# The local attention's scores: each head in its own half of the array's rows

## The chip, the cores and the metric

The kernel runs on one core of a Trainium2 chip. The metric is the time of one execution in device microseconds (us); lower is better. TensorE is written PE, its weight loads PEld, VectorE DVE, ScalarE ACT, GpSimd POOL and the queue engine SP.

## The reference, cut to what matters

One decoder layer: a mixing sub-layer of four branches (gated recurrence, dilated local attention, state-space model, cross-attention into 256 memory tokens) and a gated MLP, on 512 positions of width 1024 in float32. The change touches the local attention alone. It has twelve heads of 64 features, in three groups of four heads with (window, dilation) = (128, 1), (512, 4), (2048, 16):

```python
s = jnp.einsum('znqhe,znkhe->znhqk', qs, kb).astype(f32) * (E ** -0.5)
bias = -(slopes * dil)[:, None, None] * dist.astype(f32)
s = jnp.where(valid[None, :, None], s + bias[None, None], -jnp.inf)
m = jnp.max(s, axis=-1, keepdims=True)
p = jnp.exp(s - m)
l = jnp.sum(p, axis=-1, keepdims=True)
o = jnp.einsum('znqhk,znkhe->znqhe', p, vb.astype(f32)) / l.transpose(0, 1, 3, 2, 4)
```

The score of a query and a key of one head is thus a sum over 64 features. After the reordering by dilation there are 4 query tiles of 128 per group. In group 0 a tile sees 256 keys (the first tile 128), in groups 1 and 2 it sees 128.

## The kernel before, in words

Every large product is made in three passes to keep float32 accuracy: an operand is split by ACT and DVE into a high part (rounded to fp32r, the array's own format) and a low part (the rest), and the passes are high x high, high x low, low x high. `wload` (line 75) does that for a weight tile (`whi`, `wlo`), `split` (line 92) for an activation, `mm3` (line 83, its matmul on line 90) makes the 24 matmuls of a "unit": 128 output features by 512 positions, contracted over 8 blocks of 128.

The attention runs in two halves (`Attention(0)` and `Attention(1)`), each with two heads of every group: the 128 rows of a q, k or v unit are two heads of 64. For each group `units_v`, `units_q` and `units_k` make the units; `scores` makes the scores, their bias, maxima and exponentials; `turns` transposes the probabilities on PE (`ptr`, line 558); `values` multiplies them with v (`ops`, line 572; each head writes its own 64 rows of the bank). `run` writes the order out: scores of group g stand between the v and the q unit of group g+1, and for group 2 between units of other work (`fill`: the `glu` units in the first half, `merge` units with their `gate` and `prj` in the second). `weigh` and `combine` join the groups (`rows`, line 586; `bc`, lines 610 and 611, contracted over 2 rows).

Before the change, k is kept twice (`units_k`): with the second head's rows zeroed, and with the first head's, by a split scaled with the columns of `half` (lines 99 and 100). One score matmul (line 531) then contracts all 128 rows against both copies: the output holds both heads' scores side by side, so it has 2w columns for w keys per head. There are 3 passes per query tile. Group 0's four tiles each have a bank and an SBUF tile of their own; in groups 1 and 2 two query tiles share one bank. DVE adds the bias and takes the maximum per tile and head (line 534, with a read-out of the accumulated maximum to `col`), negates the maxima (line 541), and ACT takes the exponential (line 543).

The program takes eight PSUM banks, four under the tag `mm` (units, `ops`) and four under `ax` (scores, transposes and the rest). The program is written in one order, and a planner then orders each engine's instructions by its own estimate of when operands and buffers come free; it may put other matmuls ahead of one that still waits.

Of the kernel before, what the change touches and what calls it, by code (L numbers as in the profile page):

```python
# [12 lines left out]
F32 = mybir.dt.float32  # L13
F32R = mybir.dt.float32r
# [36 lines left out]
def _body(ctx, tc, nc, D):  # L51
# [4 lines left out]
    V, S, G, PE = nc.vector, nc.scalar, nc.gpsimd, nc.tensor  # L56

    def pool(name, bufs=1, side=None):
        return tc.tile_pool(name=name, bufs=bufs, side=side, reuse_waits="tile")
# [4 lines left out]
    def axb(name):  # L64
        return ps.tile([128, 512], F32, tag="ax", name=name)

    def f32(t):
        return t.bitcast(F32)
# [8 lines left out]
    def wload(src, n, raw=None):  # L77
        raw = wfetch(src, n) if raw is None else raw
        hi = wp.tile([128, 1024], F32R, tag="whi", name="whi")
        lo = wp.tile([128, 1024], F32R, tag="wlo", name="wlo")  # L80
        cut[:] = (S.copy(hi[:, :n], raw[:, :n]),  # L81
                  V.tensor_tensor(out=lo[:, :n], in0=raw[:, :n], in1=f32(hi[:, :n]), op=ALU.subtract))  # L82
        return hi, lo
# [9 lines left out]
    def split(hi, lo, src, scale=None, eng=V):  # L93

        if scale is None:
            a = S.copy(hi, src)
            b = eng.tensor_tensor(out=lo, in0=src, in1=f32(hi), op=ALU.subtract)
        else:
            a = S.activation(hi, src, AF.Identity, scale=scale)
            b = V.scalar_tensor_tensor(out=lo, in0=src, scalar=scale, in1=f32(hi), op0=ALU.mult, op1=ALU.subtract)  # L100
        return a, b
# [5 lines left out]
    half = cp.tile([128, 2], F32, name="half")  # L107
# [5 lines left out]
    def rstd_of(pool, s0, s1, n, tag, bufs=1, between=None, eng=V):  # L113

        t, y, e, r = (pool.tile([128, n], F32, tag=tag + x, name=tag + x, bufs=bufs) for x in "tyer")
        if s1 is None:
            eng.tensor_scalar(out=t, in0=s0, scalar1=EPS * DM, scalar2=None, op0=ALU.add)
        else:
            eng.tensor_scalar(out=t, in0=s0, scalar1=s1, scalar2=EPS * DM, op0=ALU.add, op1=ALU.add)
        S.activation(y, t, AF.Sqrt, scale=1.0 / DM)  # L120
        if between is not None:
            between()
        V.reciprocal(y, y)
        if n == 1:
            eng.tensor_scalar(out=e, in0=y, scalar1=y, scalar2=t, op0=ALU.mult, op1=ALU.mult)
        else:
            eng.tensor_tensor(out=e, in0=y, in1=y, op=ALU.mult)
            eng.tensor_tensor(out=e, in0=e, in1=t, op=ALU.mult)
        eng.tensor_scalar(out=e, in0=e, scalar1=-0.5 / DM, scalar2=1.5, op0=ALU.mult, op1=ALU.add)
        eng.tensor_tensor(out=r, in0=y, in1=e, op=ALU.mult)  # L130
        return r
# [52 lines left out]
    def t2(name, dt=F32):  # L184
        return tp.tile([128, 512], dt, tag="t2", name=name)

    def unit(u, nm):
        w = wload(D["w_in"][u], 1024)
        b = mmb(nm)
        mm3(b, w, hT, KC)  # L190
        return b


    with pool("np") as npool:
# [48 lines left out]
        for u in range(6):  # L243
            w = wk[u] if u < 3 else wload(D["mem_wk"][u], 1024)
# [5 lines left out]
            b = (axb if u % 2 else mmb)("kv")  # L250
# [7 lines left out]
        for n in range(3):  # L258
            bv = [mmb("kv") for _ in range(2)]
            for kh in range(2):  # L260
                whi, wlo = wv.pop() if wv else wload(D["mem_wv"][2 * n + kh], 1024)
                for o, passes in enumerate((((1, whi), (0, whi)), ((0, wlo),))):
                    for k in range(4):
                        cs = slice(k * 256, k * 256 + 256)
                        for t in range(2):
                            for a, w in passes:
                                done = PE.matmul(bv[t][:, :256], mT[a][:, 4 * kh + k, t * 128:(t + 1) * 128], w[:, cs],  # L267
                                                 start=(kh == k == o == 0 and a == 1), stop=(kh == 1 and k == 3 and o == 1))
# [28 lines left out]
    with pool("lru", bufs=2) as lp, pool("lruc") as lc:  # L297
# [4 lines left out]
        ab, e, s, s2, q, chf, nch = (sm("lr%d" % i) for i in range(7))  # L302
# [21 lines left out]
        for i0 in range(0, 6, 2):  # L324
            xc, gg, tr, ti = {}, {}, {}, {}
            for i in (i0, i0 + 1):
                b = unit(U_XA + i, "xa")
# [3 lines left out]
                c = xc[i] = lt("xc")  # L331
# [3 lines left out]
            for i in (i0, i0 + 1):  # L335
                b = unit(U_GA + i, "ga")
                gg[i] = lt("gg")
                S.activation(gg[i], b, AF.Gelu_apprx_tanh)
            for i in (i0, i0 + 1):
                for wt, bt, dst, nm in ((wa, ba, tr, "tr"), (wx, bx, ti, "ti")):  # L340
                    b = axb(nm)
# [19 lines left out]
        for i in range(6):  # L361
            b = unit(U_US + i, "us")
# [11 lines left out]
    for i in range(6):  # L374
        b = unit(U_XQ + i, "xq")
        split(xq[:, 0, i], xq[:, 1, i], b)
    PIECES = [[(0, 0, 128), (1, 0, 64)], [(1, 64, 64), (2, 0, 128)], [(3, 0, 128), (4, 0, 64)], [(4, 64, 64), (5, 0, 128)]]
    with pool("xap") as xp:
        for h in range(4):
            P = []  # L380
            for t0 in (0, 2):
                b = axb("xs")
                for j in range(2):
                    t = t0 + j
                    for n, (ch, p0, pn) in enumerate(PIECES[h]):
                        i = ch - (ch + 1) // 3 if pn == 128 else 4 + ch // 3 * 2 + p0 // 64
                        for o, (x, y) in enumerate(((0, 1), (1, 0), (0, 0))):
                            PE.matmul(b[:, j * 256:(j + 1) * 256], xq[:, x, ch, t * 128:(t + 1) * 128], kx[:, y, i],
                                      start=(n == 0 and o == 0), stop=(n == 1 and o == 2))
# [4 lines left out]
                p = t2("xp")  # L394
# [9 lines left out]
            for kb in range(2):  # L404
                b = axb("xpt")
                for t in range(4):
                    PE.transpose(b[:, t * 128:(t + 1) * 128], P[t // 2][:, (t % 2) * 256 + kb * 128:(t % 2) * 256 + kb * 128 + 128], ident)
                p = (t2("xpTh", F32R), t2("xpTl", F32R))
# [51 lines left out]
    ap = apx.enter_context(pool("at"))  # L460
# [6 lines left out]
    def perm_in(g, t):  # L467
        if g == 0:
            return t
        d = 4 if g == 1 else 16  # L470
        return t.rearrange("p (j r) -> p r j", r=d)

    def perm_as(g, t):
        if g == 0:
            return t
        d = 4 if g == 1 else 16
        return t.rearrange("p (r j) -> p r j", r=d)

    class Attention:
# [30 lines left out]

        def units_k(self, g):
            b = unit(U_K + 2 * g + self.h2, "k")

            t = self.k[g] = tuple(ap.tile([128, 2, 512], F32R, tag="k" + s, name="k%d%s" % (g, s), bufs=2) for s in "hl")
            for h in range(2):
                split(perm_as(g, t[0][:, h]), perm_as(g, t[1][:, h]), perm_in(g, b), scale=half[:, h:h + 1])

        def scores(self, g):
            segs = self.segs[g] = []
            if g == 0:  # L520
                parts = [[(0, 0, 128)]] + [[(t, 128 * t - 128, 256)] for t in (1, 2, 3)]
            else:
                parts = [[(t, t * 128, 128) for t in (t0, t0 + 1)] for t0 in (0, 2)]
            for prt in parts:
                new = []
                b = axb("sc")
                st = ap.tile([128, 512], F32, tag="sc", name="sc", bufs=6)
                c = 0
                for (t, k0, w) in prt:
                    for n, (x, y) in enumerate(((0, 1), (1, 0), (0, 0))):  # L530
                        PE.matmul(b[:, c:c + 2 * w].rearrange("p (h k) -> p h k", h=2), self.q[g][:, x, t * 128:(t + 1) * 128],
                                  self.k[g][y][:, :, k0:k0 + w], start=(n == 0), stop=(n == 2))
                    for h in range(2):
                        V.tensor_tensor_reduce(out=st[:, c:c + w], in0=b[:, c:c + w],
                                               in1=self.ab[g][:, h, 256 - w:256] if g == 0 else self.ab[g][:, h, :],
                                               scale=1.0, scalar=-3e38, op0=ALU.add, op1=ALU.max,
                                               accum_out=self.mcol[:, g, t, h:h + 1])
                        new.append((t, h, k0, w, st, c))
                        c += w
                t0, t1 = prt[0][0], prt[-1][0] + 1  # L540
                V.tensor_scalar(out=self.nmc[:, g, t0:t1], in0=self.mcol[:, g, t0:t1], scalar1=-1.0, scalar2=None, op0=ALU.mult)
                for (t, h, k0, w, st, c) in new:
                    S.activation(st[:, c:c + w], st[:, c:c + w], AF.Exp, bias=self.nmc[:, g, t, h:h + 1],
                                 accum_out=self.lcol[:, g, t, h:h + 1])
                segs += new
# [144 lines left out]
    with pool("wo") as wo:  # L690
# [104 lines left out]
        for u in range(3):  # L795
            w = wload(D["ffn_w_up"][u], 1024)
            b = (axb if u % 2 else mmb)("up")
# [3 lines left out]
        w = tuple(x1p.tile([128, n], F32R, name="we" + s)[:, :1024] for s, n in (("h", 1024), ("l", 1048)))  # L801
        with tc.issue_after(done.ins):
            split(*w, wfetch(D["ffn_w_up"][3]))
        b = axb("up")
# [25 lines left out]
    for i in range(24):  # L830
# [4 lines left out]
        c = fp.tile([128, 512], F32, tag="fc", name="fc", bufs=2)  # L835
# [17 lines left out]
    for kb in range(10):  # L853
        for nh in range(2):
            w = wload(D["ffn_w_down"][kb * 2 + nh], 1024)
# [15 lines left out]
    for t in range(4):  # L871
        sc = cols[:, 8 + 2 * t:10 + 2 * t]
        yg = []

        def gained(nh):
            y = fp.tile([128, 512], F32, tag="gs", name="fyg", bufs=2)
            V.tensor_tensor(out=y, in0=acc[t, nh], in1=gmo[:, nh * 512:nh * 512 + 512], op=ALU.mult)
            yg.append(y)
# [5 lines left out]
        r = rstd_of(fp, sc[:, 0:1], sc[:, 1:2], 1, "fo", 4, lambda: gained(1))  # L884
# [396 lines left out]
```

## Time and profile before

| | |
|---|---|
| median of 3 runs | 1183.03 us (1182.72 to 1184.81) |
| the profiled execution | 1185.61 us |
| its span, first to last instruction | 1183.8 us |
| PE busy | 1163.4 us, 98% of the span |
| PEld, DVE, ACT, POOL busy | 82%, 58%, 44%, 11% |
| granted TensorE clock, mean | 0.996 of 2.4 GHz |
| first and last score matmul | 442.5 us, 610.7 us |

The profiled execution lies 2.6 us above the median, and 1.8 us of it lie outside the span. "Busy" of PE counts from a matmul's start to its modelled end, and matmuls are pipelined: one of 512 columns lasts 0.389 us while the next starts 0.227 us later. How much time a matmul takes is therefore read from the chain of waits, whose pieces follow each other without overlap, or from the distance between two starts. Float32 matmuls (`ops`) leave two records each, fp32r matmuls one.

### The profile page before, as it was taken

The numbers are of one execution on the slowest core, as the hardware profiler recorded it, in microseconds if no ns is written. First come the engines' busy times: TensorE is split into PE (matmuls) and PEld (weight loads), VectorE is DVE, ScalarE is ACT, GpSimd is POOL, SyncE is SP. The second block draws the span as 40 slices with busy tenths as digits, with TensorE's granted clock in tenths as the row PEclk, the third lists the DMA queues.
The fourth block names the chain that finished last, engine by engine and source line by source line (L and its number), as shares of the span: only waits on it lengthen the run. The fifth ranks groups of instructions, "written<-read, shape, count | busy, mean of one in ns | idle before, by whom it ended". The sixth has DMA issues, their size and how long they took to land.

```text
span 1183.8 us, 15153 instructions
## 1 busy us (share of the span) xinstructions
PE 1163.4 (98%) x5786; PEld 969.0 (82%) x5786; DVE 687.7 (58%) x1249; ACT 522.8 (44%) x869; POOL 124.6 (11%) x163
## 2 busy tenths in 40 slices
PE   8999999998999999999999999999999999999997
PEld 8977788877788887888888888898888888888886
DVE  6857794588888534486447465585545444432224
ACT  6678734553434235443543234455444443422122
POOL 3000200196651000000000000010000000000000
PEclk9999999999999999999999999999999999999999
DMA  7612442213223322223122323713232323333221
GB/s 288 215 59 71 151 141 63 68 52 96 78 82 114 100 89 67 86 77 112 61 80 64 107 87 118 267 38 107 92 102 92 107 90 94 102 92 104 91 88 71
DMA packets 44296, 120.21 MB, mean 102 GB/s; under 512 B 9630, under 2 KB 13808, under 8 KB 44224
## 3 DMA queue, kind: packets, MB, share of 16 engines
q1 hardware_dynamic: 42432, 115.73, 30.1%
q0 software_dynamic: 1072, 2.46, 0.7%
q10 hardware_dynamic: 720, 1.06, 0.2%
q8 instruction: 45, 0.74, 0.2%
q14 instruction: 27, 0.22, 0.1%
HBM read 115.21 MB, written 4.01 MB: 101 GB/s over the span
## 4 chain that ended last, share of the span: by engine, by line
PE 88%; DVE 7%; DMA 1%; issue 1%; ACT 1%; POOL 1%; DVEq 0%; SPq 0%; ACTq 0%; POOLq 0%
PE up L791 22%; PE gate L90 12%; PE dn L852 11%; PE prj L90 7%; PE glu L90 4%; PE v L90 3%; PE k L90 3%; PE q L90 3%; PE xa L90 3%; PE us L90 3%; PE xq L90 3%; PE ga L90 3%; PE wo L711 2%; PE kv L267 1%; PE kv L90 1%
## 5 line engine op out<-in xcount | busy, mean ns | idle before, releaser
L82 DVE TENSOR_TENSOR wlo<-wraw,whi 128x1024 fp32r<-128x1024 f32 (+1 forms) x198 | 230.6, 1168 | 276.9 <-ACT whi L81 137.3
L81 ACT CAST whi<-wraw 128x1024 fp32r<-128x1024 f32 (+1 forms) x198 | 194.7, 986 | 332.0 <-PE dn L852 71.2
L791 PE MATMUL up<-h2l,whi 128*128 128x512 f32 (+1 forms) x400 | 148.9, 377 | 0.0
L791 PE MATMUL up<-h2h,whi 128*128 128x512 f32 (+1 forms) x400 | 148.7, 376 | 0.0
L90 PE MATMUL gate<-hTh,whi 128*128 128x512 f32 x256 | 101.1, 395 | 0.0
L90 PE MATMUL gate<-hTl,whi 128*128 128x512 f32 x256 | 100.5, 392 | 0.0
L791 PE MATMUL up<-h2h,wlo 128*128 128x512 f32 (+1 forms) x400 | 93.6, 376 | 0.0
L791 PEld LDWEIGHTS up<-h2l,whi 128*128 128x128 f32 x400 | 75.2, 188 | 13.9
L791 PEld LDWEIGHTS up<-h2h,whi 128*128 128x128 f32 x400 | 75.3, 188 | 13.8
L791 PEld LDWEIGHTS up<-h2h,wlo 128*128 128x128 f32 x400 | 72.3, 188 | 13.7
L90 PE MATMUL gate<-hTh,wlo 128*128 128x512 f32 x256 | 63.6, 389 | 0.0
L852 PE MATMUL dn<-whi,aTh 128*128 128x512 f32 x160 | 62.2, 389 | 0.0
L852 PE MATMUL dn<-whi,aTl 128*128 128x512 f32 x160 | 62.2, 389 | 0.0
L90 PEld LDWEIGHTS gate<-hTh,whi 128*128 128x128 f32 x256 | 48.1, 188 | 9.9 <-issue 0.5
L90 PEld LDWEIGHTS gate<-hTh,wlo 128*128 128x128 f32 x256 | 47.9, 188 | 9.8
L90 PEld LDWEIGHTS gate<-hTl,whi 128*128 128x128 f32 x256 | 48.1, 188 | 9.4
L841 DVE TENSOR_TENSOR fc<-fc,up 128x512 f32<-128x512 f32 x24 | 16.5, 687 | 57.6 <-PE up L791 56.5
L852 PE MATMUL dn<-wlo,aTh 128*128 128x512 f32 x160 | 39.5, 389 | 0.0
L290 DVE SCALAR_TENSOR_TENSOR th<-th,prj 128x512 f32<-128x512 f32 x24 | 16.4, 685 | 37.1 <-PE prj L90 36.8
L838 DVE SCALAR_TENSOR_TENSOR fc<-gs,fcw,fc 128x512 f32<-128x512 f32 x48 | 36.1, 751 | 1.5
L852 PEld LDWEIGHTS dn<-whi,aTl 128*128 128x128 f32 x160 | 30.0, 188 | 6.2
L852 PEld LDWEIGHTS dn<-wlo,aTh 128*128 128x128 f32 x160 | 30.0, 188 | 6.2
(517 smaller groups left out, 2439.9 us busy)
## 6 DMA issues: line engine op xcount, KB each, us to landing
wraw<-w_in SPq DMA_DIRECT2D x74, 512.0 KB, 3.5
wraw<-ffn_w_up SPq DMA_DIRECT2D x48, 512.0 KB, 3.4
wraw<-ffn_w_down SPq DMA_DIRECT2D x24, 512.0 KB, 3.5
wraw<-proj SPq DMA_DIRECT2D x24, 384.0 KB, 3.0
wraw<-ssm_glu SPq DMA_DIRECT2D x12, 384.0 KB, 3.0
wraw<-w_out SPq DMA_DIRECT2D x8, 512.0 KB, 4.3
wraw<-mem_wk SPq DMA_DIRECT2D x6, 512.0 KB, 6.8
wraw<-mem_wv SPq DMA_DIRECT2D x6, 512.0 KB, 4.2
```

Source lines behind the costliest of these rows:

```text
L81: cut[:] = (S.copy(hi[:, :n], raw[:, :n]), V.tensor_tensor(out=lo[:, :n], in0=raw[:, :n], in1=f32(hi[:, :n]), op=ALU.subtract))
L82: V.tensor_tensor(out=lo[:, :n], in0=raw[:, :n], in1=f32(hi[:, :n]), op=ALU.subtract))
L90: last = PE.matmul(out, a[:, k * 128:(k + 1) * 128], x[i][:, k], start=(n == 0), stop=(n == 3 * nk - 1))
L267: done = PE.matmul(bv[t][:, :256], mT[a][:, 4 * kh + k, t * 128:(t + 1) * 128], w[:, cs], start=(kh == k == o == 0 and a == 1), stop=(kh = ...
L290: V.scalar_tensor_tensor(out=th, in0=th, scalar=1.0, in1=b, op0=ALU.add, op1=ALU.mult)
L711: PE.matmul(b, mT[k][a][:, ts_], w[p][:, k % 2, :], start=(k == a == p == 0), stop=(k == 7 and p == 1))
L791: PE.matmul(b[:, cs], a[:, k * 128:(k + 1) * 128], x[:, k, cs], start=(n == k == 0), stop=(n == len(order) - 1 and k == KC - 1))
L838: V.scalar_tensor_tensor(out=c, in0=gs[:, j:j + 512], scalar=fcw[:, i, j:j + 1], in1=c, op0=ALU.mult, op1=ALU.add)
L841: V.tensor_tensor(out=c, in0=c, in1=bv, op=ALU.mult)
L852: PE.matmul(acc[t, nh], aT[a][:, k, ts_], w[p][:, cs], start=(k == a == p == 0), stop=(k == 23 and p == 1))
```

## The change

`units_k` makes one split without a mask, so k is kept once, with each head in its own 64 rows. In `scores` every matmul becomes two, one per head: each contracts 64 rows, given by `tile_position=(64 * h, 0)` the upper or lower half of the array's rows, and writes its w columns to that head's own bank. A part now has two banks and two SBUF tiles, one per head. Group 0 has two parts of two query tiles, groups 1 and 2 have one part of four query tiles; the number of banks taken per group is as before. The negation of the maxima is made once per part.

```diff
--- before.py
+++ after.py
@@ -510,33 +510,34 @@
 
         def units_k(self, g):
             b = unit(U_K + 2 * g + self.h2, "k")
-
-            t = self.k[g] = tuple(ap.tile([128, 2, 512], F32R, tag="k" + s, name="k%d%s" % (g, s), bufs=2) for s in "hl")
-            for h in range(2):
-                split(perm_as(g, t[0][:, h]), perm_as(g, t[1][:, h]), perm_in(g, b), scale=half[:, h:h + 1])
+            t = self.k[g] = tuple(ap.tile([128, 2, 512], F32R, tag="k" + s, name="k%d%s" % (g, s), bufs=2)[:, 0] for s in "hl")
+            split(perm_as(g, t[0]), perm_as(g, t[1]), perm_in(g, b))
 
         def scores(self, g):
             segs = self.segs[g] = []
             if g == 0:
-                parts = [[(0, 0, 128)]] + [[(t, 128 * t - 128, 256)] for t in (1, 2, 3)]
+                parts = [[(0, 0, 128), (1, 0, 256)], [(2, 128, 256), (3, 256, 256)]]
             else:
-                parts = [[(t, t * 128, 128) for t in (t0, t0 + 1)] for t0 in (0, 2)]
+                parts = [[(t, t * 128, 128) for t in range(4)]]
             for prt in parts:
                 new = []
-                b = axb("sc")
-                st = ap.tile([128, 512], F32, tag="sc", name="sc", bufs=6)
+
+                b = [axb("sc") for _ in range(2)]
+                st = [ap.tile([128, 512], F32, tag="sc", name="sc", bufs=6) for _ in range(2)]
                 c = 0
                 for (t, k0, w) in prt:
                     for n, (x, y) in enumerate(((0, 1), (1, 0), (0, 0))):
-                        PE.matmul(b[:, c:c + 2 * w].rearrange("p (h k) -> p h k", h=2), self.q[g][:, x, t * 128:(t + 1) * 128],
-                                  self.k[g][y][:, :, k0:k0 + w], start=(n == 0), stop=(n == 2))
+                        for h in range(2):
+                            r = slice(64 * h, 64 * h + 64)
+                            PE.matmul(b[h][:, c:c + w], self.q[g][r, x, t * 128:(t + 1) * 128], self.k[g][y][r, k0:k0 + w],
+                                      start=(n == 0), stop=(n == 2), tile_position=(64 * h, 0))
                     for h in range(2):
-                        V.tensor_tensor_reduce(out=st[:, c:c + w], in0=b[:, c:c + w],
+                        V.tensor_tensor_reduce(out=st[h][:, c:c + w], in0=b[h][:, c:c + w],
                                                in1=self.ab[g][:, h, 256 - w:256] if g == 0 else self.ab[g][:, h, :],
                                                scale=1.0, scalar=-3e38, op0=ALU.add, op1=ALU.max,
                                                accum_out=self.mcol[:, g, t, h:h + 1])
-                        new.append((t, h, k0, w, st, c))
-                        c += w
+                        new.append((t, h, k0, w, st[h], c))
+                    c += w
                 t0, t1 = prt[0][0], prt[-1][0] + 1
                 V.tensor_scalar(out=self.nmc[:, g, t0:t1], in0=self.mcol[:, g, t0:t1], scalar1=-1.0, scalar2=None, op0=ALU.mult)
                 for (t, h, k0, w, st, c) in new:
```

## Rows read from the trace of the kernel before

**Rows 1.** The profile page, parts 1 and 4: busy engines, the chain that ended last.

```profile
PE 1163.4 (98%) x5786; PEld 969.0 (82%) x5786; DVE 687.7 (58%) x1249; ACT 522.8 (44%) x869; POOL 124.6 (11%) x163
...
PE 88%; DVE 7%; DMA 1%; issue 1%; ACT 1%; POOL 1%; DVEq 0%; SPq 0%; ACTq 0%; POOLq 0%
```

**Rows 2.** Busy us (instructions) in one stretch: PE, PEld, DVE, ACT, POOL; clock; DMA share.

```profile
420.00:640.00 220.00, 219.91 (x1121) 179.66 (x1120) 117.27 (x239) 97.03 (x199) 2.09 (x4) 1.00 0.26 81
```

**Rows 3.** Chain, first attention half: start us, length us, engine, tile, line, count.

```profile
425.88 5.44 PE q L90 x24
...
431.76 5.49 PE k L90 x24
...
442.69 2.42 PE sc L531 x12
...
460.06 0.66 PE v L90 x2
460.72 0.37 PE ops L572 x4
461.09 5.23 PE v L90 x22
466.32 0.71 PE sc L531 x6
467.04 0.93 PE q L90 x4
467.97 0.50 PE sc L531 x3
...
480.21 1.02 PE ops L572 x16
```

**Rows 4.** Timeline, 491 to 492 us: start, length, engine, line, operation, idle before, releaser.

```profile
491.49 0.27 DVE L534 CUSTOM_DVE_ANT_0 sc<-sc,ab 128x128 f32<-128x128 f32 x1
...
491.69 0.28 DVE L534 CUSTOM_DVE_ANT_0 sc<-sc,ab 128x128 f32<-128x128 f32 x1
491.90 0.08 DVE L534 DVE_READ_ACCUMULATOR2_ANT col<- 128x1 f32 x1
...
492.04 0.19 PEld L531 LDWEIGHTS sc<-k2l,q 128*128 128x128 f32 x1 [0.51 <-DVE col L534]
```

**Rows 5.** Who waited for whom, 420 to 625 us: us in total, times, longest.

```profile
PEld sc L531 <- DVE col L534: 1.0, 3, 0.5
```

**Rows 6.** The tile ops: duration in ns min/median/max, first and last start.

```profile
L572 PE MATMUL ops<-pt,v x120: 272/273/324, 457.3 to 630.1; 128*64 128x128 f32 x120
```

**Rows 7.** Timeline of weight loads (PEld), behind ops and at bc.

```profile
459.99 0.19 PEld L90 LDWEIGHTS v<-hTh,whi 128*128 128x128 f32 x1 [0.17 <-issue]
460.10 0.19 PEld L90 LDWEIGHTS v<-hTl,whi 128*128 128x128 f32 x1
...
546.91 0.18 PEld L610 LDWEIGHTS bc<-wr,selr 2*128 2x128 f32 x1 [0.17 <-issue]
547.02 0.18 PEld L611 LDWEIGHTS bc<-wr,selr 2*128 2x128 f32 x1
```

**Rows 8.** Chain, second half, at bc.

```profile
546.99 0.42 PE bc L610
...
547.64 0.23 PE bc L610
...
548.57 5.69 PE k L90 x24
```

**Rows 9.** The tile k: splits of group 0's keys.

```profile
L99 ACT ACTIVATE k0h<-k,half x4: 688/690/692, 437.4 to 556.6; 128x512 fp32r<-128x512 f32 x4
L100 DVE SCALAR_TENSOR_TENSOR k0l<-k,half,k0h x4: 743/746/752, 438.5 to 557.4; 128x512 fp32r<-128x512 f32 x4
```

**Rows 10.** The tile xq: a split without a mask.

```profile
L96 ACT CAST xq<-xq x6: 586/589/590, 163.8 to 191.0; 128x512 fp32r<-128x512 f32 x6
L97 DVE TENSOR_TENSOR xq<-xq x6: 679/682/683, 166.5 to 192.2; 128x512 fp32r<-128x512 f32 x6
```

## The prediction

> **What bounds the kernel now.** I read the page first: PE is busy for 98% of the span and holds 88% of the chain that ended last [rows 1]. Then the stretches: from 420 to 640 us, where both attention halves run, PE is busy for 219.91 of 220 us, DVE for 117.27, ACT for 97.03, DMA a quarter [rows 2]. There the reader is to see that time moves only if PE's time does. So I took the chain of waits through the first attention half, where every piece of PE has its length [rows 3]: a unit of 24 matmuls of 512 columns is 5.44 us, 0.227 us each; the twelve score matmuls of group 0 take 2.42 us; six of 256 columns take 0.71 us, 0.118 us each. Group 0 has three of 256 and nine of 512, so one of 512 takes (2.42 - 3 x 0.118)/9 = 0.229 us. Both halves together have 54 of 256 columns and 18 of 512: 54 x 0.118 + 18 x 0.229 = 10.5 us, the whole of what the change rewrites on PE.
>
> The same rows show how they stand in PE's order: group 0's twelve lie in one piece, group 1 in pieces of six, three and three, with q matmuls between (group 2 and the second half are alike). The code says why. Two query tiles share a bank, and the third piece waits for VectorE to have read the first tile out of that bank: at 491.90 the second reduction's maximum is read out, and at 492.04 the weight load of the next score goes, after 0.51 us of idleness put down to `col` of line 534 [rows 4]. Over the stretch this wait costs 1.0 us in 3 cases [rows 5]. In group 0 each tile has a bank of its own, and there is no wait. **A bank that PE writes and DVE reads is handed over tile by tile.**
>
> **The change, part by part.**
>
> *Score matmuls.* Each becomes two, one per head, of half the columns: 18 pairs of 256 and 54 pairs of 128. That two matmuls in separate parts of the array run side by side is shown by `ops` (64 columns of the array per head): sixteen records take 1.02 us [rows 3], some 0.13 us for two with the start included, while each lasts 0.273 us [rows 6]. No row splits the array's rows between two heads, so I take the nearest. A pair of 256 should cost what one of 256 costs now, 0.118 us: 18 x (0.229 - 0.118) = **-2.0 us**. If the heads don't overlap, it is 0.236, and 18 x 0.007 = +0.1 us.
> A pair of 128 has fewer columns, but each member still needs its load of 128 columns. Two loads that start one behind the other after a stop stand 0.11 us apart, at 459.99 and 460.10 with 128 rows, at 546.91 and 547.02 with 2 rows [rows 7]: fewer rows don't shorten it. So 0.118 again, and 54 x 0 = **0**. The bounds are half of it, if the columns alone counted (54 x -0.059 = -3.2 us), and twice it, if the heads don't overlap (54 x 0.118 = +6.4 us).
> TensorE: Matmul & The Clock Gate, of the Trainium skill, section "Back-to-back issue gap", gives 81 ns for a load and a matmul of 128 columns in a stream, by which this term would be 54 x (0.081 - 0.118) = -2.0 us; the same sentence has 131 ns at 512 columns, where the trace has 227 [rows 3], so the trace decides.
>
> *Changing the array's shape.* Going from 128 x 128 to a part of the array and back isn't free. Six matmuls `bc` use 2 rows: the first takes 0.42 us in the chain where the next takes 0.23, and the k unit behind takes 5.69 us in place of 5.44 [rows 8]: 0.19 in, 0.25 out. `ops` shows it twice more: v's first two take 0.66 us in place of 0.45, the four `ops` records between 0.37 in place of 0.22, the 22 v matmuls behind 5.23 in place of 4.99 [rows 3]: 0.15 in, 0.21 to 0.24 out. A change of type alone costs nothing like it: k behind a transpose takes 5.49 [rows 3]. So each piece of scores that stands alone among whole-array matmuls costs 0.36 to 0.44 us; I take 0.40.
>
> *How many pieces.* The new parts put all four tiles of groups 1 and 2 in the same two banks, so tile 1 waits for DVE to read tile 0, tile 2 for tile 1, tile 3 for tile 2. A step is the load and matmuls (some 0.5 us), a matmul's own end, and two reductions that start 0.20 us apart [rows 4]: about 1 us, of which PE can fill more than half with other matmuls, and the planner does fill it today. So four pieces in each of groups 1 and 2. Group 0 has two parts over four banks: tiles 0 and 2 go together, then 1 and 3, singly or together: 2 or 3 pieces. That is 10 or 11 per half, 21 in all: 21 x 0.40 = **+8.4 us**. Bounds: 16 pieces at 0.36 = 5.8 us, if neighbours merge; 37 at 0.44 = 16.3 us, if each of the waiting steps falls in two.
>
> *Order within a step.* The first head's bank is free 0.20 us before the second's, so the planner may issue the first head's matmuls ahead and pairs lose their partner. Waiting steps are 3 in each of four groups and 2 in each of two: 16. Between none and two of three overlaps of 0.118 lost, I take one: 16 x 0.118 = **+1.9 us** (0 to 3.8).
>
> *Waits on DVE.* Today 8 steps wait, two in each of four groups, and lost 1.0 us [rows 5]. Sixteen lose 2.0: **+1.0 us** (0 to 2). Queued behind the waiting score on PE is the current q, glu or gate unit; behind that unit its ACT or DVE readers.
>
> *Keys.* A split with a mask is 2 ACT of 0.690 and 2 DVE of 0.746 us per unit [rows 9]; without it one of 0.589 and one of 0.682, as `xq` shows [rows 10]. Six units: 4.7 us of ACT and 4.9 us of DVE less. Both engines are half idle there [rows 2], so **0**; at best the 1.0 us of waits goes (-1.0), and nothing is lost. The negation of the maxima comes half as often, also beside PE. The exponentials of the first tiles now wait for the fourth's maximum, about 2 us later; the transposes behind them come a whole q unit (5.44 us) later, so they stay covered; if not, PE would stop for up to 2 us per group. No DMA changes.
>
> **Sum:** -2.0 + 0 + 8.4 + 1.9 + 1.0 + 0 = +9.3 us, against the profiled execution's span of 1183.8 us, 1185.6 with what lies around it; that execution is 2.6 us above the median of the three runs shown, and I set the difference on the median: 1183.0 + 9.3 = **1192.3 us**.
>
> **The rivals.**
> *The half arrays pay (faster).* If row halves doubled the rate of loads as well as matmuls, the 10.5 us would become 5.25, a gain of 5.25; it decides once the pieces are fewer than 5.25/0.40 = 13. With two pieces per group, 12 in all, and PE filling nothing, 1183.0 - 5.25 + 4.8 = 1182.6; with one piece per group and DVE keeping up, 1183.0 - 5.25 + 2.4 = 1180.2. For it: `ops` overlaps fully. Against it: the load's 0.11 us [rows 7], and the handover of banks that the third piece of group 1 shows [rows 3 to 5]. The Trainium skill, TensorEngine Tiling, "Theoretical Speedup", gives up to 2x for a dimension of at most 64, which is this rival. Chance 0.07, and 0.08 for an outcome within 0.2%, in between: costs of shape and gain cancel, 1181 to 1185 us.
> *The heads come apart.* Other matmuls get in between the heads of each waiting step: 37 pieces (16.3) and two overlaps lost (3.8) with the waits (1.0) and the gain of group 0's unsplit pairs alone (6 x 0.111 = 0.7): +20.4, 1203.4 us; half of that, about 1198. Chance 0.17.
> *The change does not do what it says:* the two heads run one after the other. +6.4 + 0.1 + 8.4 + 1.0 = +15.9, 1198.9 us. Nothing in `ops` speaks for it, but no row shows row halves. Chance 0.07.
> The forecast holds the rest, 0.61.
>
> **How the numbers follow.** About 0.2% is what a measurement of this kernel can tell from no change. Faster by more than that: 0.06, the first rival's lower end; within 0.2%: 0.09; slower: 0.85. The likeliest case alone spans 1187 to 1197 (pieces from 16 to 24, order from 0 to 3.8). The range goes down to 1184.5, into the cancelling case, and up to 1202 for the rivals above.
>
> **What would show it.** In the new trace: score matmuls with 64 rows, a pair's two starts some 0.01 us apart and pairs 0.12 us apart, for 128 as for 256 columns; ten or more separate pieces of scores per half in the chain, each with 0.15 to 0.2 us lost at its start and 0.2 to 0.25 behind it; ACT and DVE some 5 us less busy each. Wrong would be: pairs of 128 at 0.06 us (then -3 us), score pieces in one run per group, or heads' starts 0.1 us apart throughout. If PE shows gaps of microseconds ahead of transposes, the exponentials were late and my covering argument fell.

## The result and the profile after

The changed kernel takes 1195.81 us (median of 4 runs, 1195.2 to 1196.5), the kernel before, run beside it, 1183.92 us (1182.72 to 1185.38): ratio 1.0101, 95% interval 1.0089 to 1.0113 (here and below over all runs, so not exactly the quotient of the medians). It is 11.9 us slower. The forecast was 9.3 us slower, 1192.3 us; the measured time lies inside its range. The profiled execution took 1195.89 us, its span is 1194.1 us.

The page, parts 1 and 4, answers to [rows 1]:

```profile
PE 1171.6 (98%) x5858; PEld 969.4 (81%) x5858; DVE 683.3 (57%) x1235; ACT 518.4 (43%) x863; POOL 125.2 (10%) x163
...
PE 91%; DVE 4%; issue 1%; DMA 1%; ACT 1%; POOL 1%; SPq 0%; DVEq 0%; ACTq 0%; POOLq 0%
```

PE has 72 more instructions, the second heads. DVE and ACT are 4.4 us less busy each, the keys' part. PE is again "busy" for 98%; that share can't show where 11.9 us went. The stretch that holds most of both attention halves shows more; it answers to [rows 2] (us, then PE, PEld, DVE, ACT, POOL busy, clock, DMA share, GB/s):

```profile
420.00:640.00 220.00, 216.13 (x1124) 171.08 (x1124) 100.37 (x210) 87.81 (x186) 2.09 (x4) 0.99 0.25 79
```

PE now stands idle for 3.87 us where it stood for 0.09, and the granted clock has a dent. To place all of it I measured the first half from its first v matmul to the first `rows`, and the second from the last `glu` to the last `rows`: 89.47 and 96.24 us before, 96.60 and 101.82 us after, **+12.7 us** together. Behind the attention the two traces agree; ahead of it the changed kernel's profiled execution was 2.5 us shorter with the same order on PE, a spread between executions that the runs before show too (1182.72 to 1185.38).

The chain of waits through the first half answers to [rows 3] (start, length, engine, tile, line, count):

```profile
440.32 0.43 DVE wlo L82
...
441.47 0.28 DVE sc L535
...
441.81 1.07 PE sc L532 x9
442.88 0.89 PE q L90 x3
443.77 0.91 PE sc L532 x6
...
466.75 0.76 PE sc L532 x6
467.51 0.67 PE q L90 x2
468.17 0.48 PE sc L532 x6
468.65 0.67 PE q L90 x2
469.32 0.49 PE sc L532 x6
```

Three things are to be seen. The scores of a group are now cut into pieces with other matmuls between (two or three q matmuls in the lines shown): group 0 stands in two pieces of 18 and 6 matmuls, groups 1 and 2 in four pieces of six (three pairs). That is 20 pieces in all, where the kernel before has 13. Two q matmuls between pieces take 0.67 us where two take 0.45 inside a unit. And the chain, which in [rows 3] ran through PE, now goes over DVE: a `wlo` (a weight split of other work), then a reduction, then the score that waited.

Who waited for whom, 420 to 650 us, answers to [rows 5]:

```profile
PEld sc L532 <- DVE col L535: 9.0, 14, 1.3
...
PE sc L532 <- DVE col L535: 3.8, 6, 0.9
```

1.0 us in 3 cases has become 9.0 us in 14 (the second row is the same waits, seen by the matmul). The timeline of group 2, which answers to [rows 4], shows why one of them is long (start, length, engine, line, operation, idle before, releaser):

```profile
490.43 0.39 PE L532 MATMUL sc<-k2h,q 64*128 64x128 f32 x4
490.43 0.96 DVE L82 TENSOR_TENSOR wlo<-wraw,whi 128x768 fp32r<-128x768 f32 x1 [3.12 <-PE glu L90]
491.31 1.05 DVE L654 SCALAR_TENSOR_TENSOR gz<-gth,glu 128x512 f32<-128x512 f32 x1
492.20 0.28 DVE L535 CUSTOM_DVE_ANT_0 sc<-sc,ab 128x128 f32<-128x128 f32 x1
...
492.40 0.29 DVE L535 CUSTOM_DVE_ANT_0 sc<-sc,ab 128x128 f32<-128x128 f32 x1
492.54 0.39 PEld L532 LDWEIGHTS sc<-k2l,q 64*128 64x128 f32 x2 [1.26 <-DVE col L535]
492.54 0.54 PE L532 MATMUL sc<-k2l,q 64*128 64x128 f32 x2 [0.82 <-DVE col L535]
...
493.05 0.69 DVE L100 SCALAR_TENSOR_TENSOR ycl<-gz,ych 128x512 fp32r<-128x512 f32 x1 [0.36 <-ACT ych L99]
493.66 0.29 DVE L535 CUSTOM_DVE_ANT_0 sc<-sc,ab 128x128 f32<-128x128 f32 x1
```

The first tile's scores are done before 491 us, but their reduction stands in DVE's order behind `wlo` and `gz`, which take 0.96 and 1.05 us. PE waits 0.82 us, and at the next tile `ycl` stands ahead in the same way. The waiting pair starts in two steps (two matmuls last 0.54 us together, one 0.32): first one head, 0.21 us later the other, as DVE reads out the one bank and then the other.

Last, the windows behind it, with the clock (columns as above):

```profile
490.00:495.40 5.40, 4.52 (x29) 2.71 (x27) 3.89 (x15) 1.23 (x2) 0.00 (x0) 1.00 0.25 73
495.40:498.80 3.40, 3.40 (x13) 2.73 (x13) 0.68 (x5) 1.85 (x10) 0.54 (x1) 0.51 0.12 36
```

For 3.4 us the granted clock is 0.51, the lower of its two levels, 1.2 GHz. The trace of before has no such dip in the attention (clock 1.00 in [rows 2]). Matmuls of 512 columns start 0.427 us apart in the dip, not 0.227, so about 1.6 us go there (3.4 x (1 - 0.227/0.427)).

### The profile page after: what moved, and what is told of

The parts are those of the page before. It is cut to its first block, busy times and chain, and to the rows that moved or that the text cites. A ratio compares the mean times of both kernels' runs of the same rounds, so it can differ in the third digit from the quotient of the medians.

```text
span 1194.1 us, 15264 instructions
## 1 busy us (share of the span) xinstructions
PE 1171.6 (98%) x5858; PEld 969.4 (81%) x5858; DVE 683.3 (57%) x1235; ACT 518.4 (43%) x863; POOL 125.2 (10%) x163
## 4 chain that ended last, share of the span: by engine, by line
PE 91%; DVE 4%; issue 1%; DMA 1%; ACT 1%; POOL 1%; SPq 0%; DVEq 0%; ACTq 0%; POOLq 0%
PE up L792 22%; PE gate L90 13%; PE dn L853 11%; PE prj L90 8%; PE glu L90 4%; PE q L90 3%; PE k L90 3%; PE xa L90 3%; PE us L90 3%; PE xq L90 3%; PE ga L90 3%; PE v L90 3%; PE wo L712 2%; PE kv L267 1%; PE xo L415 1%
## 5 line engine op out<-in xcount | busy, mean ns | idle before, releaser
L842 DVE TENSOR_TENSOR fc<-fc,up 128x512 f32<-128x512 f32 x24 | 16.5, 688 | 57.0 <-PE up L792 55.8
L290 DVE SCALAR_TENSOR_TENSOR th<-th,prj 128x512 f32<-128x512 f32 x24 | 16.5, 686 | 36.2 <-PE prj L90 35.9
L853 PEld LDWEIGHTS dn<-whi,aTh 128*128 128x128 f32 x160 | 30.0, 188 | 6.2
```

The lines of the kernel that those rows point to most:

```text
L290: V.scalar_tensor_tensor(out=th, in0=th, scalar=1.0, in1=b, op0=ALU.add, op1=ALU.mult)
L842: V.tensor_tensor(out=c, in0=c, in1=bv, op=ALU.mult)
L853: PE.matmul(acc[t, nh], aT[a][:, k, ts_], w[p][:, cs], start=(k == a == p == 0), stop=(k == 23 and p == 1))
```

## The experiments

The theory after this reading: the loss is pieces plus waits for the handover of a bank (PE writes a tile, DVE reads it, PE may write the next). Its rivals: half-array matmuls themselves are dear; the heads' order loses their overlap; the key part matters. For each kernel "scores" is the time that score matmuls cost on PE over all six groups: the time from the matmul ahead to the third behind, less 0.2267 us (5.44/24) for every other matmul in it. Before it is 11.3 us, after 23.1 us. The first tool is to put all matmuls of a part ahead of its reads, which takes away every wait inside a part.

**All reads behind the matmuls, in the changed kernel.**

```diff
                                       start=(n == 0), stop=(n == 2), tile_position=(64 * h, 0))
+                    c += w
+                c = 0
+                for (t, k0, w) in prt:
                     for h in range(2):
                         V.tensor_tensor_reduce(
```

> The changed kernel with all score matmuls of a part ahead of the first DVE reduction of that part, so that no matmul waits for a bank to be read; 6 pieces in PE's order. Theory H: the scores cost their stream alone, 54 pairs of 128 at 0.109 and 18 pairs of 256 at 0.118 us = 8.0 us, and 6 pieces at 0.35 = 2.1 us: 10.1 us against 11.3 in the kernel before, so about 1.2 us faster than before (0.998 to 1.000 of it), some 13 us below the changed kernel. Rival S (the half-array matmuls themselves or their pairing are slow): stays 5 us or more above the kernel before. Rival L (the exponentials, now later, become the wait): PE stops ahead of the transposes, about 2 us per group, +5 to +10 us.

Measured: 1182.55 us (11 runs) against 1183.0, ratio 0.9995 (0.9986 to 1.0004), 13 us below the changed kernel. The chain has one piece per group:

```profile
440.67 1.60 PE sc L532 x24
463.71 1.49 PE sc L532 x24
487.09 1.49 PE sc L532 x24
```

Scores cost 10.4 us, and the halves take 88.85 and 96.04 us, 0.8 us less than before. So half arrays with one piece per group cost nothing against the kernel before; the whole loss hangs on reads that stand between the matmuls of a part.

**The same in the kernel before.** (The same three lines, with `c += 2 * w`.)

> The kernel before with all score matmuls of a part ahead of the part's first reduction: 6 pieces in place of 13, no wait for a bank. Theory H: only the waits of the kernel before go, 0.3 us of PE's time by the starts of its matmuls, at most the 1.0 us that the waits name: 0.2 to 1.0 us faster, within what can be told from no change. Rival L (later exponentials become the wait): slower by 1 us or more.

Measured: 1182.47 us (11 runs) against 1183.0, 0.9994 (0.9986 to 1.0003). Scores cost 10.6 us instead of 11.3: the handover's whole price before was 0.7 us. Between this kernel and the last, the half arrays change PE's stream by -0.2 us: they save 2.4 us in matmuls and pay about 2.1 us for six pieces of another shape (at the price per piece that the next experiment finds).

**The price of a piece.** In the kernel of the first experiment, groups 0 and 1 are written by hand into the q unit in four pieces, without a wait. `score_steps` (not printed) returns four steps, each with the six matmuls of one query tile; all reads stand behind the fourth.

```diff
...
         for n, (a, i, k) in enumerate(order):
+            if n % 2 == 0 and n // 2 < len(between):
+                between[n // 2]()
             last = PE.matmul(out, a[:, k * 128:(k + 1) * 128], x[i][:, k], ...)
...
-            b = unit(U_Q + 2 * g + self.h2, "q")
+            b = unit(U_Q + 2 * g + self.h2, "q", self.score_steps(g - 1) if g else ())
...
                 self.units_v(g)
-                if g:
-                    self.scores(g - 1)
                 self.units_q(g)
```

> As e2_reads_last (no wait for a bank), but the scores of groups 0 and 1 are written out by hand as four pieces of one query tile each, with two q matmuls between, as the changed kernel has them: 18 pieces in place of 6, no waits. Theory (a piece costs 0.35 us of PE by the change of the array's shape): 12 x 0.35 = 4.2 us, 1186.7 us. Rival (pieces cost only the waits behind them): 1182.5 us.

Measured: 1187.03 us (5 runs) against 1183.72, 1.0033 (1.0021 to 1.0046). The chain:

```profile
464.32 0.48 PE sc L579 x6
465.46 0.48 PE sc L579 x6
466.60 0.48 PE sc L579 x5
467.74 0.48 PE sc L579 x6
```

Pieces start 1.14 us apart where three pairs (0.33) and two q matmuls (0.45) would be 0.78: 0.36 each. The halves (90.98 and 98.19) are 4.28 us longer for 12 more pieces, **0.357 us a piece**. In the changed kernel's trace it splits into 0.09 us ahead of the first pair, 0.05 ahead of the second, 0.09 and 0.11 ahead of the first two matmuls behind.

**Whole arrays in the changed order.** Banks, parts and reads as changed, but each head contracts 128 rows against masked keys.

```diff
...
-            split(perm_as(g, t[0]), perm_as(g, t[1]), perm_in(g, b))
+            for h in range(2):
+                split(perm_as(g, t[0][:, h]), perm_as(g, t[1][:, h]), perm_in(g, b), scale=half[:, h:h + 1])
...
-                            PE.matmul(b[h][:, c:c + w], self.q[g][r, x, t * 128:(t + 1) * 128], self.k[g][y][r, k0:k0 + w],
-                                      start=(n == 0), stop=(n == 2), tile_position=(64 * h, 0))
+                            PE.matmul(b[h][:, c:c + w], self.q[g][:, x, t * 128:(t + 1) * 128], self.k[g][y][:, h, k0:k0 + w],
+                                      start=(n == 0), stop=(n == 2))
```

> The changed kernel's banks, parts and order of PE (20 pieces, the same counts), but every score matmul contracts all 128 rows against the masked copy of its head's keys, as before, so the array keeps its shape. What is taken away: the change of shape and the overlap of the two heads. Theory H with the shape price of 0.35 us per piece: 20 x 0.35 = 7.0 us less, 72 matmuls more in sequence at about 0.115 = 8.3 us more, partners lost no longer matter, 3 us less: -3 to +2 us against the changed kernel, +9 to +13 against before; in the trace the starts into and out of a piece lose their 0.09 to 0.11 us gaps, and the waits on DVE stay at 4 us or more. Rival (changing shape costs nothing, the gaps at the pieces are the bank waits): the gaps of 0.09 us into and 0.20 us out of each piece stay.

Measured: 1195.94 us (4 runs) against 1183.0, 1.0111 (1.0097 to 1.0125), as slow as the changed kernel by another sum. There are two whole-array matmuls for one pair: 108 of 128 columns, 0.1125 us apart, and 36 of 256, 0.12 us apart, make 16.5 of the 23.3 us that the scores cost. Little is lost where a piece ends: the last score and the first matmul behind it take 0.11 and 0.28 us from start to start, in the changed kernel 0.20 and 0.34. The other 6.8 us are, but for some 0.06 us at the end of a piece, the same waits, in the same 14 and 6 cases:

```profile
PEld sc L532 <- DVE col L535: 7.3, 14, 1.3
...
PE sc L532 <- DVE col L535: 3.3, 6, 0.8
```

So the waits belong to banks and reads, not to the half array.

**Two parts of two tiles in groups 1 and 2.**

```diff
-                parts = [[(t, t * 128, 128) for t in range(4)]]
+                parts = [[(t, t * 128, 128) for t in (t0, t0 + 1)] for t0 in (0, 2)]
```

> The changed kernel with groups 1 and 2 in two parts of two query tiles (four banks) as group 0 has them, in place of one part of four tiles (two banks). In PE's order the score pieces go from 20 to 12 and the steps that wait for a bank from 16 to 12. Theory H (the handover of the banks between PE and DVE makes most of the loss: waits on DVE, 4.4 us more than before in the changed kernel's trace, partners lost in the waiting steps, about 3 us, and the pieces it forces, 0.35 us each): 8 pieces fewer save 2.8 us; one wait per group remains, about 1.15 us as group 0 of the changed kernel shows it, so waits hardly change: +8 to +10 us against the kernel before. Rival S (the narrow matmuls themselves are slower, whatever their order): still +11 to +12.5 us. Rival C (a dip of the granted clock, seen once in the changed kernel's trace, makes a good part): within 1 us of the changed kernel in runs without it.

Measured: 1200.07 us (4 runs) against 1183.0, 1.0139 (1.0123 to 1.0154). A miss: this was to be better than the change and is 4 us worse. There are 12 pieces as expected, but the second tile of each part still waits for the reads of the first, and PE has fewer other matmuls to put into these waits:

```profile
PEld sc L532 <- DVE col L535: 9.6, 9, 1.9
PE sc L532 <- DVE col L535: 7.1, 7, 1.5
```

Nine waits cost more than fourteen. And the clock falls twice in the first half, each time behind a stretch in which PE stood idle for 0.72 or 1.95 us. At 0.227 us against 0.427 the two falls (10.2 us) take some 4.8 us. That is 3.2 more than the one in the changed kernel's trace, and most of the 4.6 us by which the halves (100.49 and 102.55 us) are longer than there:

```profile
465.00:469.90 4.90, 4.18 (x29) 2.92 (x27) 2.29 (x13) 1.61 (x3) 0.00 (x0) 1.00 0.15 33
469.90:476.70 6.80, 6.78 (x21) 5.40 (x21) 0.87 (x7) 3.11 (x16) 0.54 (x1) 0.50 0.15 56
...
495.00:500.60 5.60, 3.65 (x29) 2.77 (x29) 4.44 (x20) 2.62 (x9) 0.00 (x0) 1.00 0.22 70
500.60:504.00 3.40, 3.40 (x10) 2.66 (x9) 0.20 (x3) 1.90 (x10) 0.54 (x1) 0.50 0.17 46
```

**The heads one behind the other.** The kernel of the first experiment with the loop over heads outside the loop over passes, so that a head's three matmuls stand together in PE's order.

```diff
-                    for n, (x, y) in enumerate(((0, 1), (1, 0), (0, 0))):
-                        for h in range(2):
+                    for h in range(2):
+                        for n, (x, y) in enumerate(((0, 1), (1, 0), (0, 0))):
```

> As e2_reads_last, but in each query tile the three passes of the first head stand ahead of the three of the second, in place of alternating. It tests whether the two halves of the array run side by side. If they do and PE issues in order, a second head's first matmul joins the first head's last, so a tile takes 5 steps where e2 has 3... counted as starts: the tile grows by one step where the next tile's first head can join too, 24 tiles x 0.11 = 2.6 us, or two steps where it cannot, 5.2 us: 1185 to 1188 us. If the halves never run side by side, alternating brought nothing and the time stays that of e2 (1182.5 us).

Measured: 1182.48 us (10 runs) against 1183.72, 0.9994 (0.9985 to 1.0003). A miss: the lost overlap doesn't show at all. The timeline of group 1:

```profile
466.25 0.33 PE L532 MATMUL sc<-k1l,q 64*128 64x128 f32 x2
466.41 0.40 PE L532 MATMUL sc<-k1h,q 64*128 64x128 f32 x4
466.63 0.28 PE L532 MATMUL sc<-k1l,q 64*128 64x128 f32 x2
466.75 0.39 PE L532 MATMUL sc<-k1h,q 64*128 64x128 f32 x4
```

In PE's order a `k1l` is followed by two `k1h`, then by the second head's `k1l`. On the chip the two `k1l` start together (0.33 us for both, 0.32 for the first alone), then all four `k1h`: each half of the array runs on through its own matmuls, and which head comes first within a tile made no difference.

**Twice the matmuls, 64 keys each.** The kernel of the first experiment; each matmul of 128 keys becomes two.

```diff
+                    v = 64 if w == 128 else w
+                    for j in range(0, w, v):
...
-                            PE.matmul(b[h][:, c:c + w], ..., self.k[g][y][r, k0:k0 + w],
+                                PE.matmul(b[h][:, c + j:c + j + v], ..., self.k[g][y][r, k0 + j:k0 + j + v],
```

> As e2_reads_last, but each pair of matmuls over 128 keys is made as two pairs over 64 keys, the same products and one more weight load per head. Theory W (a pair of 128 costs its weight load, 0.109 us): 54 pairs more at 0.109 = 5.9 us, 1188.4 us. Rival (it costs its columns): pairs of 64 take half, 0 us more, 1182.5 us.

Measured: 1190.7 us (4 runs) against 1183.72, 1.006 (1.0045 to 1.0076). The chain and, below, the windows around the third group:

```profile
463.65 2.80 PE sc L534 x48
```

```profile
488.30:491.80 3.50, 3.50 (x52) 3.37 (x52) 2.68 (x4) 1.23 (x2) 0.00 (x0) 1.00 0.36 109
491.80:495.20 3.40, 3.40 (x9) 2.66 (x9) 1.81 (x17) 1.52 (x8) 0.54 (x1) 0.50 0.07 19
```

Twenty-four pairs of 64 columns take 2.80 us where twelve of 128 took 1.49: the twelve more cost 1.31 us, 0.109 us each, so half the columns save nothing. The pace is that of two loads, 0.11 us apart [rows 7]; that the load sets it is inferred from this match and not shown. No run changes the columns of the scores' loads, and the transposes of `rows`, whose loads have 34 columns, also start 0.11 us apart. Four such groups and 0.34 us more in each group 0 (1.94 us for 30 matmuls against 1.60) make +5.9 us. The halves (93.42 and 100.59 us) are 9.1 us longer; the other 3.2 us fit two dips of the clock at 1.6 us, here with PE busy throughout ahead of them.

**The key part alone.** The kernel of the first experiment with keys masked and doubled as in the kernel before (the split of the whole-array experiment); the matmul reads its head's copy, `self.k[g][y][r, h, k0:k0 + w]`.

> As e2_reads_last, but the keys stay masked and doubled (two splits with a mask per k unit) and each half of the array reads its head's copy: the part of the change that touches ACT and DVE, undone alone. Forecast of the prediction: hidden beside PE, so the time of e2_reads_last (1182.5 us), although ACT and DVE are busy for some 4.7 and 4.9 us more. Rival: the shorter splits helped e2, then 1183.5 us or more.

Measured: 1181.99 us (10 runs) against 1183.5, 0.9986 (0.9977 to 0.9996). 420 to 640 us, with masked keys:

```profile
420.00:640.00 220.00, 220.00 (x1195) 178.88 (x1194) 117.53 (x233) 96.88 (x199) 2.09 (x4) 1.00 0.26 83
```

DVE and ACT are busier by 4.9 and 4.4 us than without (112.66 and 92.52), the halves take 88.87 and 96.06 us: not longer.

**The clock in a second execution.** The changed kernel, the two-part kernel and the whole-array kernel, unchanged, one run each.

> The changed kernel once more, for a second look at the granted clock. If its fall to half in the first half's group 2 belongs to the kernel, it comes again, some 1.6 us of the loss; if it was chance, the clock stays at 1.0 from 420 to 650 us and the attention takes about 1.6 us less than in the first profile.

> The two-part kernel once more. Its first profile had the clock at half for 6.8 and 3.4 us, behind the longest waits of PE. If waits of this length bring the clock down, it falls again in one or both places; if not, the time comes out some 5 us lower, near 1195 us.

> The whole-array kernel once more: it waits as long as the changed kernel but its pieces keep the array busier. If the clock's fall needs the thinner use of the array as well as the waits, the clock stays at 1.0 as in its first profile; if waits alone bring it, a fall shows this time.

Measured: 1196.7, 1203.44 and 1195.45 us against 1183.5. The changed kernel has its dip in the same group again, for 6.8 us instead of 3.4; the two-part kernel has four, 17 us in all. The whole-array kernel has none, in either execution, though its PE stands idle as long in that group (0.84 us, 0.82 in the changed kernel):

```profile
490.00:495.00 5.00, 4.16 (x25) 3.11 (x23) 3.38 (x11) 1.60 (x3) 0.00 (x0) 1.00 0.27 90
495.00:500.00 5.00, 5.00 (x28) 4.22 (x27) 1.19 (x9) 2.58 (x13) 0.54 (x1) 1.00 0.10 31
```

**A mixed version.** Reads last; half arrays and plain keys only for group 0, where they save matmul time; groups 1 and 2 as before. The cut shows the keys and the parts, against the changed kernel.

```diff
...
+            if g == 0:
+                split(t[0][:, 0], t[1][:, 0], b)
+                return
+            for h in range(2):
+                split(perm_as(g, t[0][:, h]), perm_as(g, t[1][:, h]), perm_in(g, b), scale=half[:, h:h + 1])
...
-                parts = [[(t, t * 128, 128) for t in range(4)]]
+                parts = [[(t, t * 128, 128) for t in (t0, t0 + 1)] for t0 in (0, 2)]
```

> All score matmuls of a part ahead of its reductions, group 0 on half arrays with unmasked keys (scores 1.81 us per half in e2_reads_last against 2.42 on the whole array), groups 1 and 2 on the whole array with masked keys (1.45 us in e5_before_reads_last against 1.69 on half arrays). The scores then cost 2 x 1.81 + 4 x 1.45 = 9.4 us, against 11.3 in the kernel before: 1.9 us faster than before, 1181.1 us, 0.9984 of it. If the later exponentials or the keys' splits matter, nothing of it shows.

Measured: 1182.63 us (11 runs) against 1183.72, 0.999 (0.9982 to 0.9999). In the trace the halves take 88.34 and 95.52 us, 1.85 us less than before, as expected; the runs give 1.1. It is the best order on PE that was found, and no more than 0.2% faster than the kernel before.

## Why the prediction came out right, and where it was off

The direction, the bound (time moves only with what PE does or waits for) and the order of the terms by size held; the sum was 3.4 us short of the +12.7 of the traces, and 2.6 short of the 11.9 of the medians. Part of this nearness is luck: pieces were priced 1.3 us too high, against waits 3.5 us too low and 1.6 us of the clock that stood in no term. The terms, by the experiments:

| step | forecast, us | found, us | from |
|---|---|---|---|
| streams of pairs | -2.0 | -2.4 | first two experiments, six pieces taken off |
| pieces | 21 x 0.40 = +8.4 | 20 x 0.357 = +7.1 | hand-written pieces |
| waits on DVE and order within a step | 1.0 + 1.9 = +2.9 | +6.4 | what is left of scores, 23.1 - 8.2 - 7.1 - 0.7 of the dip = 7.1, less 0.7 before |
| keys | 0 | 0 | masked keys |
| clock | none | +1.6 | windows |

The part of the dip that falls into scores is read from group 2: its last piece and the three matmuls behind take 1.75 us in the first half, in the dip, and 1.05 in the second. The whole-array run comes near the 7.1 us by another way, with its 6.8. The terms found add to 12.7, by which the halves differ.

**Pairs.** The rows named for it are there: matmuls of 64 rows, a pair's starts a few nanoseconds apart, pairs of 256 columns 0.118 us apart. Pairs of 128 are 0.109 apart, near the 0.11 us between two loads [rows 7], not 0.118: 54 x 0.009 = 0.5, about the extra -0.4. The Trainium skill, TensorE: Matmul & The Clock Gate, section "Back-to-back issue gap", gives 81 ns for a matmul of 128 columns with its load. This case has 109 ns for a pair, also at 64 columns, and 112 ns in the whole-array run, so that figure is not borne out here.

**Pieces.** Ten per half, as forecast (10 or 11; the kernel before has 13 and not 14, since in group 1 of the second half the two pieces of three stand together), each at the lower bound of its price (0.36 us) and under the 0.44 us of `bc` [rows 8]. This term alone outweighs what the half arrays save.

**Waits: the step that failed.** "A step is ... about 1 us, of which PE can fill more than half with other matmuls, and the planner does fill it today." In groups 1 and 2 the pieces start 1.14 to 2.87 us apart: in front of the reduction stands whatever DVE has in its order, a `wlo` of 0.96 or 1.23 us, `gz`, `ycl`. The sum took the 0.125 us per step that the kernel before loses (1.0 us in 8 steps) and applied it to twice the steps; but there one tile in a part had to wait, and now in groups 1 and 2 three tiles in a row do. Four single waits (1.26 us from start to start in group 0 of both halves, 0.99 and 0.67 beyond a matmul's 0.227 in group 2), less the 0.1 us that a pair takes anyway, come to 3.8 us, more than half of the term. No run changes DVE's order alone, so how the rest divides between work ahead of the reduction and the handover itself is not shown. **The order of heads** was put beside it as a loss of partners; with the heads one behind the other nothing was lost, so the mechanism is refuted. What is real in it is the 0.21 us between the two heads' starts behind a wait.

**Keys and exponentials** were right: no idle time of PE stands ahead of a transpose, and the 4.4 us of each engine are worth nothing beside a full PE.

**The clock** was not in the sum. The range covers it by its margin only. By the same working the fall of 6.8 us in the second execution costs 3.2 us.

**The rivals.** Half arrays did not pay twofold against the kernel before: from pair to pair the loads stay 0.109 us apart, as single loads do [rows 7]. With one piece per group and no wait the stream goes from 10.6 to 8.2 us, and the change of shape takes that back. The Trainium skill, TensorEngine Tiling, section "Theoretical Speedup", gives up to 2x for a dimension of at most 64. The runs bear that out against whole-array matmuls of one head each: 144 of them make 16.5 us in the whole-array run, the 72 pairs 8.2. The kernel before had no such factor left to give, because one of its matmuls, with masked keys and 256 columns in 0.12 us, already did what a pair does. The heads did not come apart into 37 pieces, and they do run side by side.

## What to carry to other kernels

Where PE writes several tiles into one bank and another engine reads them out, put all matmuls of that bank ahead of the first read, or give each tile a bank, as group 0 of the kernel before does without a wait: a handover costs not the read alone but all that stands ahead of it in the reader's order. Before splitting the array, ask what one whole-array matmul already does. Here the split paid only in group 0, with 256 keys per tile and one piece (1.81 us against 2.42); with 128 keys, where a pair takes the 0.109 us that it takes with 64, it lost (1.69 against 1.45). Count pieces and price them (0.36 us here) before counting columns. A PE that is "98% busy" on both sides can hide 12 us; measure the stage by its starts.

## What was not expected of the hardware

The two halves of the array do not keep the program's order between each other: matmuls three places apart in PE's order start together (0.33 us for both). A wait of one half still holds up what is queued behind it: in the changed kernel's group 2 the first head's second matmul starts 0.215 us behind its first, as soon as the other head's wait is over, and 0.160 us behind it where nobody waits.

The granted clock can fall to 1.2 GHz in the middle of a kernel for 3.4 or 6.8 us. It fell in the changed kernel (both executions), the two-part kernel (two and four times) and the 64-key kernel (twice), always behind half-array scores; ahead of it PE had stood idle for some 0.7 us or more, or had run 48 matmuls of 64 columns in a row. It did not fall in the whole-array kernel with the same waits, nor in the half-array kernels without waits and with 128 columns; nor did it fall behind the waits in the changed kernel's group 0, in which PE stood idle for 0.93 us. What decides it was not settled.

A change of array shape costs 0.357 us there and back, though on both sides stand fp32r matmuls that write all 128 rows of a bank.
